# Gate product in plain float32 over four column groups, and a new table of stage offsets

## The chip, the cores and the metric

The kernel runs on one core of one Trainium2 chip. The core has a matrix engine (TensorE, PE in the profile, with its weight loads as PEld), a vector engine (VectorE, DVE), a scalar engine (ScalarE, ACT), GpSimd (POOL), and SyncE (SP), which here issues the loads and stores. The metric is device time in microseconds (us), lower is better. The kernel before took 2730.89 us, the median of three runs (2729.17 to 2732.62).

## The reference

One layer of a decoder over 2048 tokens of width 1024 in float32: a gated DeltaNet mixer with 8 heads of 128 and chunks, a memory cross-attention with 4 heads beside it, an output projection, a layer norm, an MLP with squared ReLU and 4096 hidden units, and a second layer norm. What matters here is the gate part: 16 of the columns of the input projection, 8 for `a` and 8 for `b`.

```python
def gdn_mixer(x, mem_k, mem_v, w_in, conv_w, a_log, dt_bias, gate_norm_w, w_out):
    proj = x @ w_in
    qkv = proj[..., :3 * GDN_WIDTH]
    z = proj[..., 3 * GDN_WIDTH:4 * GDN_WIDTH]
    a = proj[..., 4 * GDN_WIDTH:4 * GDN_WIDTH + GDN_HEADS]
    b = proj[..., 4 * GDN_WIDTH + GDN_HEADS:4 * GDN_WIDTH + 2 * GDN_HEADS]
    ...
    beta = jax.nn.sigmoid(b.astype(jnp.float32))
    g = -jnp.exp(a_log) * jax.nn.softplus(a.astype(jnp.float32) + dt_bias)
    o = chunk_gated_delta_rule(q, k, v, g, beta)
```

## The kernel before, in words

The tokens are worked through in four blocks of 512 (TB), two blocks to a pass s. For each pass the main loop (line 1809) runs `mixer` for both blocks, then `out_seven` (output projection and first norm), `ff1` and `ff2` (the MLP and second norm). Matrices of 1024 rows are handled in eight pieces k of 128 rows (KT = 8).

**Precision.** The large products run on float32r operands (a float32 type that the matmul reads at reduced precision). To keep float32 accuracy, `split` (line 555) writes each operand as a high part, by a copy on ScalarE, and a low part, by a subtraction on VectorE; `mm3` (line 573) then issues three matmuls: high·high, high·low, low·high. The split tokens of a block are the tiles T (line 649): 4 high and 4 low tiles of two k each, all eight buffers of the tag `tt`. The next block's T can be written only as the present block's last product with T has read them. Products of the recurrence (`pc`, `po` in `gdn_b`, line 1064) and transposes are plain float32.

**The order of the work.** Nothing is issued directly. Every call on an engine is recorded by `Recorder` (line 206) with a cost (line 272), the buffers that it needs and what it depends on. `issue` (line 313) then goes through all recorded operations on a modelled clock: at each engine the one that is ready and has the lowest priority number goes next; the number is the order of recording plus `shift` plus `base`. `spot` (line 529) sets `base` from the table `PLACE` (line 190), which holds an offset for some stages, named by block, step and letter (B and A are the two halves of the recurrence of a head, D its projections, Z its gate z, M memory attention, F a part of the MLP, X and W operands and weights of the output projection). A buffer of a tag is given out in the order of its users' first recorded use. The modelled clock decides the order alone; the times here are all from the chip.

**The gate product.** `gates(b, T)` (line 726) loads the 16 columns of weights (`abraw`), splits them into high and low halves side by side in `abw`, a stationary tile of 32 columns, and issues for each k two matmuls, against the high and the low part of T:

```python
            nc.tensor.matmul(a[:32], w[:, k], T_of(T, 0, k), start=k == 0, stop=False)
            nc.tensor.matmul(a[:32], w[:, k], T_of(T, 1, k), start=False, stop=k == KT - 1)
```

The result `aab` has 32 rows by 512 tokens: the products with the high weights and with the low weights. It is copied out by ScalarE (`ab`), transposed in four pieces to tokens by 32 (`pab`), and the two halves of 16 columns are added into `gab`. The rest of `gates` works out the decay and beta from it; that part is not changed.

**Where it stands.** For block 0 the tokens come in `first_tokens` (line 1587), piece by piece, each with its split, into two-piece tiles of the tag `tok`; `columns` loads the norm weights, and `gates` follows (line 1820). For the later blocks `next_block(b, step)` (line 1608) runs steps 0 to 4: steps 0 to 3 load two k of x each (`xj`, a buffer of the tag `wraw`, of which there are three) and split them into T; step 4 loads the first weights and calls `gates`. For odd blocks (1 and 3) these steps are recorded behind the mixer of the block before; for block 2 they are recorded in `ff2` of the first pass, during its last product (line 1561), whose own operands are in slots of the tags `d` (11 buffers) and `s0` (14 buffers).

Of the kernel before, what the change touches and what calls it, by code (L numbers as in the profile page):

```python
# [8 lines left out]
F32 = mybir.dt.float32  # L9
# [5 lines left out]
P = 128  # L15
# [4 lines left out]
H = 8  # L20
# [164 lines left out]
class Op:  # L185
# [2 lines left out]


PLACE = {  # L190
# [12 lines left out]
}  # L203


class Recorder:
# [65 lines left out]
    def cost(o, name, wr, rd, args, kw):  # L272
# [3 lines left out]
        if e == "PE":  # L276
            rhs = kw.get("rhs", args[2])
            mo, n = _prod(args[1].shape[1:]), _prod(rhs.shape[1:])
            f32 = name == "transpose" or isinstance(rhs, Ref) and rhs.buf.dtype == F32
            o.load, o.cols, o.lhs = 4 + 0.84 * mo, mo, args[1].buf if isinstance(args[1], Ref) else None  # L280
            o.last = 2.4 + 0.8334 * n if f32 else 13.4 + 0.4167 * n
            if name == "transpose":
                return o.last
            if f32:
                return o.last + max(o.last, o.load)
            return o.last
# [154 lines left out]
def hybrid_layer(  # L441
# [46 lines left out]
    def small(name, shape, bufs=3, dt=F32):  # L488
        return rec.buf(sm, shape, dt, name, bufs, name)
# [42 lines left out]
    state = [rec.buf(cst, (P, P), F32, "state%d" % h, 1, "state") for h in range(H)]  # L532
    for h in range(H):
        nc.gpsimd.memset(state[h], 0.0)
    lnc = rec.buf(cst, (P, 4 * KT), F32, "lnc", 1, "lnc")
    nea = rec.buf(cst, (P, H), F32, "nea", 1, "nea")
    halo = rec.buf(cst, (P, 24, 3), F32, "halo", 1, "halo")
# [185 lines left out]
                                  in_=st[i].bitcast(F32).rearrange("p (h e) -> p h e", h=MH))  # L723


    def gates(b, T):
        raw = small("abraw", [P, KT, 16], 1)
        nc.sync.dma_start(out=raw, in_=w_ab.rearrange("p (k f) -> p k f", k=KT))
        w = small("abw", [P, KT, 32], 1, F32R)
        split(raw, w[:, :, :16], w[:, :, 16:])  # L730
        a = bank("aab", "acc")
        for k in range(KT):
            nc.tensor.matmul(a[:32], w[:, k], T_of(T, 0, k), start=k == 0, stop=False)
            nc.tensor.matmul(a[:32], w[:, k], T_of(T, 1, k), start=False, stop=k == KT - 1)
        ab = slot("ab", "th")
        nc.scalar.copy(out=ab[:32], in_=a[:32])
        pab = bank("pab", "m")
        for c in range(NC):
            nc.tensor.transpose(pab[:, c * 32:(c + 1) * 32], ab[:32, c * P:(c + 1) * P], ident[:32, :32])
        pc = pab[:, :P].rearrange("p (c f) -> p f c", c=NC)  # L740
        pv = small("gab", [P, 16, NC], 1)
        nc.vector.tensor_copy(pv, pc[:, 16:])
        nc.vector.tensor_tensor(out=pv, in0=pc[:, :16], in1=pv, op=ALU.add)
        sh = [P, H, NC]
        if b == 0:
            alog = small("alog", [P, H], 1)
# [838 lines left out]
        nc.vector.tensor_copy(lnc, pt[:, :4 * KT])  # L1585

    def first_tokens():
        T = T_tiles()
        rt = rec.buf(wp, (P, KT, P), F32, "wraw", NR, "wraw")
        wt, hi, lo = pair()  # L1590
        hi, lo = hi.rearrange("p (k f) -> p k f", k=KT), lo.rearrange("p (k f) -> p k f", k=KT)
        for k in range(KT):
            if k % 2 == 0:
                xj = tok_tile("xj").rearrange("p (k f) -> p k f", k=2)
            if k in W0K:
                w = slice(k, W0K[k])
                kw = range(k, W0K[k])
                nc.sync.dma_start(out=rt[:, w].part(*kw), in_=w_in[0].rearrange("p (k f) -> p k f", k=KT)[:, w])
                split(rt[:, w].part(*kw), hi[:, w].part(*kw), lo[:, w].part(*(100 + i for i in kw)))
            xk = xj[:, k % 2].part(k % 2)  # L1600
            nc.sync.dma_start(out=xk, in_=xtd[:, k, 0:TB])
            split(xk, T_of(T, 0, k), T_of(T, 1, k))
        nc.sync.dma_start(out=wsc[0], in_=wt.bitcast(F32))
        return T, ([hi[:, k].part(k) for k in range(KT)], [lo[:, k].part(100 + k) for k in range(KT)])

# [2 lines left out]
    def next_block(b, step):  # L1608

        if b >= NB:  # L1610
            return
        if step < 4:
            if step == 0:
                ahead["T"] = T_tiles()
            k = 2 * step
            xj = rec.buf(wp, (P, 1024), F32, "wraw", NR, "xj").rearrange("p (k f) -> p k f", k=2)
            nc.sync.dma_start(out=xj, in_=xtd[:, k:k + 2, b * TB:(b + 1) * TB])
            split(xj, *(t[step] for t in ahead["T"]))
        else:
            ahead["w0"] = load_in(b, 0)  # L1620
            ahead["G"] = gates(b, ahead["T"])


    def mixer(b, T, w0, G):
# [184 lines left out]
    for s in range(NB // 2):  # L1809
        x1d = [rec.buf(dr, (P, D), F32, "x1d%d" % t, 1, "x1d") for t in range(2 * NC)]  # L1810
        T0d = rec.buf(dr, (P, KT, TB), F32, "T0d", 1, "T0d")
        for n in ("A11", "A12", "A22", "S1", "S2", "S3", "S4"):
            xo[n] = rec.buf(dr, (P, 6, TB), F32, "xo" + n, 1, "xo")
        inv = inverse_tiles()
        for i in range(2):
            b = 2 * s + i
            if b == 0:
                T, w0 = first_tokens()
                columns()
                G = gates(b, T)  # L1820
            else:
                T, w0, G = ahead["T"], ahead["w0"], ahead["G"]
            mixer(b, T, w0, G)
            if i == 0:
                for k in range(5):
                    next_block(b + 1, k)
        ys, T = out_seven(s, x1d, T0d)
        ff1(s, ys, T0d, first_half(T))
        ff2(s, x1d)
# [56 lines left out]
```

## Time and profile before

| | |
|---|---|
| median of three runs | 2730.89 us |
| the profiled execution's own time | 2731.02 us |
| its span, first to last instruction | 2729.3 us |
| TensorE busy, matmuls | 2707.3 us (99%), 13605 records |
| TensorE weight loads | 2265.5 us (83%) |
| VectorE busy | 2106.6 us (77%) |
| ScalarE busy | 1634.3 us (60%) |
| GpSimd busy | 414.5 us (15%) |
| mean granted TensorE clock | 0.999 |

The profile is one execution recorded by the hardware. Its page gives busy time for each engine and the chain of work that ended last; views of the trace give groups of instructions, what an engine waited for, the timeline of instructions, and busy time in chosen stretches. Rows of the timeline merge neighbours of one kind: start, length from the first start to the last end, engine, line, operation, output<-inputs, shape, count, and in brackets how long the engine sat idle before and what ended that. As all operations pass through the recorder, they all show its line 424, so they are told apart by the names of their tiles. Numbers of a group `x64: 387/396/479` are least, median and greatest duration in ns. float32r operands show as f32 on TensorE.

### The profile page before, as it was taken

The numbers are of one execution on the slowest core, as the hardware profiler recorded it, in microseconds if no ns is written. First come the engines' busy times: TensorE is split into PE (matmuls) and PEld (weight loads), VectorE is DVE, ScalarE is ACT, GpSimd is POOL, SyncE is SP. The second block draws the span as 40 slices with busy tenths as digits, with TensorE's granted clock in tenths as the row PEclk, the third lists the DMA queues.
The fourth block names the chain that finished last, engine by engine and source line by source line (L and its number), as shares of the span: only waits on it lengthen the run. The fifth ranks groups of instructions, "written<-read, shape, count | busy, mean of one in ns | idle before, by whom it ended". The sixth has DMA issues, their size and how long they took to land.

```text
span 2729.3 us, 42448 instructions
## 1 busy us (share of the span) xinstructions
PE 2707.3 (99%) x13605; PEld 2265.5 (83%) x13605; DVE 2106.6 (77%) x5644; ACT 1634.3 (60%) x4106; POOL 414.5 (15%) x1030
## 2 busy tenths in 40 slices
PE   9999999999999999999999999999999999999998
PEld 7888888888888888888888888888887888888887
DVE  7999889998877777655778887888878666567575
ACT  7778767776475555333446676777756655553341
POOL 3233223321000000000023221332201000000000
PEclk9999999999999999999999999999999999999999
DMA  8666548867787879765754445345678643476673
GB/s 321 232 222 229 206 177 293 309 244 267 264 307 282 296 271 311 261 219 194 263 212 147 140 163 185 140 147 173 217 264 287 228 165 137 162 277 224 212 237 114
DMA packets 208543, 613.99 MB, mean 225 GB/s; under 512 B 23072, under 2 KB 32192, under 8 KB 188352
## 3 DMA queue, kind: packets, MB, share of 16 engines
q1 hardware_dynamic: 207888, 611.23, 63.7%
q8 instruction: 107, 1.75, 0.3%
q14 instruction: 116, 0.95, 0.1%
q10 hardware_dynamic: 432, 0.05, 0.0%
HBM read 436.54 MB, written 174.65 MB: 224 GB/s over the span
## 4 chain that ended last, share of the span: by engine, by line
PE 92%; DVE 3%; ACT 3%; POOL 1%; issue 1%; DMA 1%; DVEq 0%; SPq 0%; POOLq 0%; ACTq 0%
PE f2A L424 13%; PE fA L424 13%; PE ao L424 8%; PE f2C L424 6%; PE fC L424 6%; PE av L424 6%; PE aq L424 6%; PE ak L424 6%; PE az L424 5%; PE f2B L424 3%; PE fB L424 3%; PE amq L424 3%; PE pc L424 3%; PE po L424 2%; PE pkq L424 2%; PE pq L424 1%
## 5 line engine op out<-in xcount | busy, mean ns | idle before, releaser
L424 DVE TENSOR_TENSOR whl<-wraw,whl 128x512 fp32r<-128x512 f32 (+2 forms) x294 | 257.0, 884 | 112.5 <-ACT whl L424 109.6
L424 ACT CAST whl<-wraw 128x512 fp32r<-128x512 f32 (+2 forms) x294 | 226.6, 780 | 158.6 <-PE fC L424 54.6
L424 PE MATMUL fA<-B,whl 128*128 128x512 f32 x1152 | 278.9, 389 | 0.0
L424 ACT CAST X<-X 128x1024 fp32r<-128x1024 f32 x118 | 123.9, 1052 | 231.2 <-DMA X<-xsc 203.2
L424 PE MATMUL f2A<-whl,X 128*128 128x512 f32 x1152 | 262.1, 389 | 0.0
L424 PEld LDWEIGHTS fA<-B,whl 128*128 128x128 f32 x1152 | 216.1, 188 | 45.3 <-DVE B L424 0.3
L424 PEld LDWEIGHTS f2A<-whl,X 128*128 128x128 f32 x1152 | 216.3, 188 | 44.8
L424 DVE TENSOR_TENSOR X<-X,X 128x1024 fp32r<-128x1024 f32 x118 | 144.0, 1221 | 128.8 <-ACT X L424 128.8
L424 PE MATMUL aq<-T,whl 128*128 128x512 f32 x768 | 216.5, 409 | 6.5 <-ACT T L424 5.5
L424 PE MATMUL av<-T,whl 128*128 128x512 f32 x768 | 221.9, 405 | 1.0 <-DVE Bc L424 1.0
L424 PE MATMUL az<-T,whl 128*128 128x512 f32 x768 | 222.8, 404 | 0.0
L424 PE MATMUL ak<-T,whl 128*128 128x512 f32 x768 | 210.8, 405 | 0.0
L424 PE MATMUL fC<-B,whl 128*128 128x512 f32 x768 | 186.8, 389 | 0.4 <-DVE B L424 0.4
L424 PE MATMUL f2C<-whl,X 128*128 128x512 f32 x768 | 174.7, 389 | 0.0
L424 PEld LDWEIGHTS fC<-B,whl 128*128 128x128 f32 x768 | 144.0, 188 | 31.0 <-DVE B L424 0.8
L424 PEld LDWEIGHTS f2C<-whl,X 128*128 128x128 f32 x768 | 144.2, 188 | 29.9
L424 PEld LDWEIGHTS aq<-T,whl 128*128 128x128 f32 x768 | 136.8, 191 | 28.7 <-ACT T L424 5.5
L424 PEld LDWEIGHTS av<-T,whl 128*128 128x128 f32 x768 | 137.8, 189 | 24.2 <-ACT mst L424 1.4
L424 PEld LDWEIGHTS ak<-T,whl 128*128 128x128 f32 x768 | 137.3, 189 | 23.5
L424 PEld LDWEIGHTS az<-T,whl 128*128 128x128 f32 x768 | 137.9, 189 | 22.3
L424 POOL TENSOR_SCALAR ve<-mv 128x1 f32<-128x1 f32 x34 | 16.8, 493 | 918.3 <-DVE mv L424 917.8
L424 PE MATMUL ao<-whl,X 128*128 128x512 f32 x528 | 139.9, 404 | 0.3 <-DVE whl L424 0.3
(294 smaller groups left out, 6294.3 us busy)
## 6 DMA issues: line engine op xcount, KB each, us to landing
whl<-wsc SPq DMA_DIRECT2D x108, 1024.0 KB, 4.9
wraw<-in_w_ff_dram SPq DMA_DIRECT2D x106, 512.0 KB, 4.4
X<-xsc SPq DMA_DIRECT2D x96, 512.0 KB, 3.9
wsc<-whl SPq DMA_DIRECT2D x36, 1024.0 KB, 6.5
whl<-tsc SPq DMA_DIRECT2D x64, 512.0 KB, 4.6
xsc<-hB SPq DMA_DIRECT2D x96, 256.0 KB, 3.8
xo<-cat SPq DMA_DIRECT2D x80, 256.0 KB, 4.3
wraw<-in_w_in_dram SPq DMA_DIRECT2D x35, 512.0 KB, 6.0
```

The lines of the kernel that those rows point to most:

```text
L424: o.fn(*[res(a) for a in o.args], **{k: res(v) for k, v in o.kw.items()})
```

## The change

The gate product takes x itself instead of its split. The weights `abw` are one constant tile, 8 pieces of 32 columns in plain float32, cleared once; the 16 columns are loaded once in `first_tokens`, and the other 16 of each piece stay zero. `gate_rows` issues one matmul for each k, and writes it to the output rows 32·(k mod 4) to 32·(k mod 4) + 31 of `aab`, which puts it on another group of 32 columns of the array for each of four neighbouring k; k and k + 4 accumulate in the same rows. `gates` then copies all 128 rows, transposes four full 128 by 128 pieces, and adds the four groups by a reduction for each piece.

For block 0 `first_tokens` records all eight matmuls behind the splits. In `next_block`, odd blocks load x as before and record the matmuls in two batches of four, at steps 1 and 3; block 2 loads each k by itself into a slot of the tag `s0` and records all eight in one batch at step 3. The bank of `aab` is asked for at step 0. The cost function gets a line for such matmuls, a quarter of the usual float32 cost. `PLACE` is replaced as a whole.

```diff
--- before.py
+++ after.py
@@ -188,18 +188,19 @@
 
 
 PLACE = {
-    ('w',): 445, (0, 0, 'F'): -65, (0, 1, 'Y'): 285, (0, 2, 'D'): -5, (0, 2, 'Y'): -225, (0, 2, 'n'): 600,
-    (0, 5, 'A'): 175, (0, 5, 'M'): -20, (0, 6, 'A'): -145, (0, 6, 'B'): -200, (0, 6, 'D'): 90, (0, 6, 'Z'): 325,
-    (0, 7, 'B'): -600, (0, 7, 'D'): -170, (0, 8, 'B'): -430, (1, 2, 'D'): 335, (1, 3, 'A'): 150, (1, 3, 'B'): 300,
-    (1, 3, 'D'): 245, (1, 3, 'K'): -185, (1, 4, 'A'): -160, (1, 5, 'A'): 160, (1, 5, 'Z'): 210, (1, 6, 'A'): 45,
-    (1, 6, 'B'): -550, (1, 6, 'D'): -165, (1, 6, 'F'): -45, (1, 7, 'Z'): -60, (2, 1, 'Z'): -60, (2, 3, 'A'): 340,
-    (2, 4, 'A'): 10, (2, 5, 'A'): -40, (2, 5, 'B'): 100, (2, 5, 'M'): -140, (2, 6, 'D'): -600, (2, 6, 'M'): 120,
-    (2, 7, 'A'): 10, (2, 7, 'D'): 295, (2, 8, 'A'): -10, (2, 8, 'B'): -225, (2, 8, 'M'): -100, (2, 8, 'Z'): -440,
-    (3, 2, 'A'): -195, (3, 2, 'B'): -530, (3, 2, 'D'): 360, (3, 3, 'B'): 235, (3, 3, 'D'): 140, (3, 3, 'Z'): -110,
-    (3, 4, 'A'): 25, (3, 4, 'B'): 250, (3, 5, 'A'): -460, (3, 5, 'D'): 20, (3, 5, 'Z'): -80, (3, 6, 'D'): 70,
-    (3, 6, 'Z'): 20, (3, 7, 'B'): -315, (3, 7, 'Z'): 315, (3, 8, 'Z'): 115, (0, 0, 2, 'X'): 150, (0, 1, 0, 'X'): 140,
-    (0, 5, 1, 'X'): 225, (0, 5, 2, 'X'): 155, (0, 6, 0, 'W'): -150, (1, 0, 0, 'W'): -355, (1, 1, 2, 'W'): -600,
-    (1, 5, 0, 'X'): 10, (1, 5, 2, 'W'): -375, (1, 6, 0, 'W'): 15, (1, 6, 2, 'X'): -25,
+    (0, 0, 'F'): -410, (0, 0, 'H'): -270, (0, 1, 'D'): -120, (0, 1, 'H'): -130, (0, 1, 'Y'): -75, (0, 1, 'Z'): -130,
+    (0, 12, 'F'): 160, (0, 13, 'F'): 50, (0, 2, 'A'): 340, (0, 2, 'D'): -235, (0, 2, 'n'): 215, (0, 3, 'A'): -285,
+    (0, 3, 'Z'): -165, (0, 4, 'Z'): 25, (0, 5, 'D'): 125, (0, 5, 'F'): 55, (0, 5, 'M'): -25, (0, 5, 'Z'): -400,
+    (0, 6, 'A'): 40, (0, 6, 'F'): 10, (0, 6, 'M'): -165, (0, 7, 'A'): 125, (0, 7, 'M'): 80, (0, 7, 'Z'): 105,
+    (0, 8, 'A'): 300, (0, 9, 'B'): 235, (0, 9, 'F'): -150, (1, 2, 'A'): -295, (1, 3, 'K'): 205, (1, 3, 'Z'): 320,
+    (1, 4, 'B'): -160, (1, 4, 'D'): 15, (1, 4, 'K'): -595, (1, 4, 'O'): 495, (1, 4, 'Z'): -35, (1, 5, 'B'): 215,
+    (1, 5, 'D'): 20, (1, 5, 'O'): 390, (1, 5, 'Z'): -40, (1, 6, 'M'): 345, (1, 6, 'O'): 245, (1, 6, 'Z'): -215,
+    (1, 7, 'D'): 20, (1, 7, 'M'): 50, (1, 7, 'Z'): -215, (1, 9, 'B'): -130, (2, 1, 'D'): -25, (2, 1, 'Z'): -60,
+    (2, 2, 'A'): 190, (2, 2, 'D'): 75, (2, 2, 'Z'): -355, (2, 3, 'A'): -110, (2, 3, 'B'): 20, (2, 5, 'A'): 245,
+    (2, 5, 'D'): 110, (2, 5, 'M'): 190, (2, 6, 'Z'): -220, (2, 7, 'A'): -180, (2, 7, 'M'): 325, (2, 8, 'B'): -360,
+    (2, 8, 'Z'): 445, (3, 1, 'A'): 90, (3, 1, 'D'): -175, (3, 2, 'B'): -400, (3, 5, 'M'): -10, (3, 6, 'B'): -220,
+    (3, 6, 'Z'): -105, (3, 7, 'A'): -60, (3, 7, 'B'): 40, (0, 4, 0, 'W'): -600, (1, 4, 2, 'X'): -300,
+    (1, 5, 1, 'W'): -160, (1, 6, 0, 'W'): 180, (1, 6, 1, 'W'): -375,
 }
 
 
@@ -281,6 +282,8 @@
             o.last = 2.4 + 0.8334 * n if f32 else 13.4 + 0.4167 * n
             if name == "transpose":
                 return o.last
+            if f32 and mo == 32 and n == 512:
+                return (o.last + max(o.last, o.load)) / 4
             if f32:
                 return o.last + max(o.last, o.load)
             return o.last
@@ -532,6 +535,8 @@
     state = [rec.buf(cst, (P, P), F32, "state%d" % h, 1, "state") for h in range(H)]
     for h in range(H):
         nc.gpsimd.memset(state[h], 0.0)
+    abw = rec.buf(cst, (P, KT, 32), F32, "abw", 1, "abw")
+    nc.gpsimd.memset(abw, 0.0)
     lnc = rec.buf(cst, (P, 4 * KT), F32, "lnc", 1, "lnc")
     nea = rec.buf(cst, (P, H), F32, "nea", 1, "nea")
     halo = rec.buf(cst, (P, 24, 3), F32, "halo", 1, "halo")
@@ -723,24 +728,21 @@
                                   in_=st[i].bitcast(F32).rearrange("p (h e) -> p h e", h=MH))
 
 
-    def gates(b, T):
-        raw = small("abraw", [P, KT, 16], 1)
-        nc.sync.dma_start(out=raw, in_=w_ab.rearrange("p (k f) -> p k f", k=KT))
-        w = small("abw", [P, KT, 32], 1, F32R)
-        split(raw, w[:, :, :16], w[:, :, 16:])
-        a = bank("aab", "acc")
-        for k in range(KT):
-            nc.tensor.matmul(a[:32], w[:, k], T_of(T, 0, k), start=k == 0, stop=False)
-            nc.tensor.matmul(a[:32], w[:, k], T_of(T, 1, k), start=False, stop=k == KT - 1)
+    def gate_rows(a, xs, ks):
+        for k, x in zip(ks, xs):
+            q = slice(32 * (k % 4), 32 * (k % 4) + 32)
+            nc.tensor.matmul(a[q], abw[:, k], x, start=k < 4, stop=k >= 4)
+
+    def gates(b, a):
         ab = slot("ab", "th")
-        nc.scalar.copy(out=ab[:32], in_=a[:32])
+        nc.scalar.copy(out=ab, in_=a)
         pab = bank("pab", "m")
         for c in range(NC):
-            nc.tensor.transpose(pab[:, c * 32:(c + 1) * 32], ab[:32, c * P:(c + 1) * P], ident[:32, :32])
-        pc = pab[:, :P].rearrange("p (c f) -> p f c", c=NC)
+            nc.tensor.transpose(pab[:, c * P:(c + 1) * P], ab[:, c * P:(c + 1) * P], ident)
         pv = small("gab", [P, 16, NC], 1)
-        nc.vector.tensor_copy(pv, pc[:, 16:])
-        nc.vector.tensor_tensor(out=pv, in0=pc[:, :16], in1=pv, op=ALU.add)
+        for c in range(NC):
+            nc.vector.tensor_reduce(out=pv[:, :, c], in_=pab[:, c * P:(c + 1) * P].rearrange("p (j f) -> p f j", j=4)[:, :16],
+                                    op=ALU.add, axis=AX.X)
         sh = [P, H, NC]
         if b == 0:
             alog = small("alog", [P, H], 1)
@@ -1585,7 +1587,7 @@
         nc.vector.tensor_copy(lnc, pt[:, :4 * KT])
 
     def first_tokens():
-        T = T_tiles()
+        T, xs = T_tiles(), []
         rt = rec.buf(wp, (P, KT, P), F32, "wraw", NR, "wraw")
         wt, hi, lo = pair()
         hi, lo = hi.rearrange("p (k f) -> p k f", k=KT), lo.rearrange("p (k f) -> p k f", k=KT)
@@ -1600,6 +1602,10 @@
             xk = xj[:, k % 2].part(k % 2)
             nc.sync.dma_start(out=xk, in_=xtd[:, k, 0:TB])
             split(xk, T_of(T, 0, k), T_of(T, 1, k))
+            xs.append(xk)
+        nc.sync.dma_start(out=abw[:, :, :16], in_=w_ab.rearrange("p (k f) -> p k f", k=KT))
+        ahead["ab"] = bank("aab", "acc")
+        gate_rows(ahead["ab"], xs, range(KT))
         nc.sync.dma_start(out=wsc[0], in_=wt.bitcast(F32))
         return T, ([hi[:, k].part(k) for k in range(KT)], [lo[:, k].part(100 + k) for k in range(KT)])
 
@@ -1611,14 +1617,28 @@
             return
         if step < 4:
             if step == 0:
-                ahead["T"] = T_tiles()
+                ahead["T"], ahead["x"], ahead["ab"] = T_tiles(), [], bank("aab", "acc")
             k = 2 * step
-            xj = rec.buf(wp, (P, 1024), F32, "wraw", NR, "xj").rearrange("p (k f) -> p k f", k=2)
-            nc.sync.dma_start(out=xj, in_=xtd[:, k:k + 2, b * TB:(b + 1) * TB])
-            split(xj, *(t[step] for t in ahead["T"]))
+            c = slice(b * TB, (b + 1) * TB)
+            if b % 2:
+                xj = rec.buf(wp, (P, 1024), F32, "wraw", NR, "xj").rearrange("p (k f) -> p k f", k=2)
+                nc.sync.dma_start(out=xj, in_=xtd[:, k:k + 2, c])
+                split(xj, *(t[step] for t in ahead["T"]))
+                ahead["x"] += [xj[:, j] for j in range(2)]
+                batch = 4
+            else:
+                for j in range(2):
+                    xj = slot("xj", "s0")
+                    nc.sync.dma_start(out=xj, in_=xtd[:, k + j, c])
+                    split(xj, *(T_of(ahead["T"], i, k + j).part(j) for i in range(2)))
+                    ahead["x"].append(xj)
+                batch = KT
+            n = len(ahead["x"])
+            if n % batch == 0:
+                gate_rows(ahead["ab"], ahead["x"][n - batch:], range(n - batch, n))
         else:
             ahead["w0"] = load_in(b, 0)
-            ahead["G"] = gates(b, ahead["T"])
+            ahead["G"] = gates(b, ahead["ab"])
 
 
     def mixer(b, T, w0, G):
@@ -1817,7 +1837,7 @@
             if b == 0:
                 T, w0 = first_tokens()
                 columns()
-                G = gates(b, T)
+                G = gates(b, ahead["ab"])
             else:
                 T, w0, G = ahead["T"], ahead["w0"], ahead["G"]
             mixer(b, T, w0, G)
```

## The prediction

> **What bounds the kernel now.** I read the page first, then stretches of the span, then the waits of TensorE.
>
> ```profile
> span 2729.3 us, 42448 instructions
> PE 2707.3 (99%) x13605; PEld 2265.5 (83%) x13605; DVE 2106.6 (77%) x5644; ACT 1634.3 (60%) x4106; POOL 414.5 (15%) x1030
> PE 92%; DVE 3%; ACT 3%; POOL 1%; issue 1%; DMA 1%; DVEq 0%; SPq 0%; POOLq 0%; ACTq 0%
> ```
>
> TensorE (PE) is busy for 99% of the span, and 92% of the chain that ended last is its own instructions. So a matmul that goes away is worth what it occupied, and one that comes costs the same, wherever it stands. Next, busy time by stretch; the columns are the length, then PE, PEld, DVE, ACT, POOL, the clock.
>
> ```profile
> 14.00:320.00 306.00, 302.01 (x1704) 255.97 (x1702) 273.09 (x966) 238.69 (x730) 97.91 (x233) 1.00 0.68 243
> 320.00:690.00 370.00, 369.13 (x2093) 312.98 (x2092) 330.43 (x1223) 258.48 (x853) 98.21 (x245) 1.00 0.73 257
> 690.00:1360.00 670.00, 669.30 (x2978) 551.80 (x2977) 481.83 (x686) 344.37 (x508) 17.48 (x34) 1.00 0.77 267
> 1360.00:1680.00 320.00, 320.00 (x1772) 271.75 (x1771) 254.49 (x948) 204.47 (x701) 91.05 (x237) 1.00 0.46 166
> 1680.00:2050.00 370.00, 369.68 (x2065) 314.95 (x2064) 314.05 (x1179) 248.66 (x815) 86.45 (x224) 1.00 0.54 190
> 2050.00:2718.00 668.00, 666.63 (x2968) 550.65 (x2968) 435.58 (x610) 331.50 (x488) 15.12 (x28) 1.00 0.59 205
> ```
>
> PE's idle time between 14 and 2718 us is 3.99 + 0.87 + 0.70 + 0 + 0.32 + 1.37 = 7.25 us. That is all an order of the work could still win by closing gaps, so it bounds from above what the new table of offsets gives. The rest of the 22 us of idle time lies in the first load and in the last tokens' normalization, which the change leaves alone. The clock column is 1.00 throughout.
>
> **What is removed.** The gate product, tile aab, is 64 matmuls on a stationary tile of 32 columns.
>
> ```profile
> L424 PEld LDWEIGHTS aab<-T,abw x64: 107/108/112, 13.4 to 1673.5; 128*32 128x32 f32 x64
> L424 PE MATMUL aab<-T,abw x64: 387/396/479, 13.6 to 1673.7; 128*32 128x512 f32 x64
> L424 ACT COPY ab<-aab x4: 575/576/577, 17.6 to 1674.1; 32x512 f32<-32x512 f32 x4
> ```
>
> A duration of 396 ns is not a cost: it includes the way through the array, which overlaps the next matmul. The cost is the distance between starts, and the timeline gives it where the 16 stand together, at the end of the MLP ahead of block 2:
>
> ```profile
> 1358.67 0.39 PE L424 MATMUL f2A<-whl,xl 128*128 128x512 f32 x1
> 1358.67 3.53 PEld L424 LDWEIGHTS aab<-T,abw 128*32 128x32 f32 x16
> 1358.90 3.82 PE L424 MATMUL aab<-T,abw 128*32 128x512 f32 x16
> 1362.55 0.61 PE L424 MATMUL f2A<-whl,xh 128*128 128x512 f32 x2
> ```
>
> From 1358.90 to 1362.55 is 3.65 us, 0.228 us each. In block 0 the same 16 stand from 13.64 to 17.38, which is 3.74 us:
>
> ```profile
> 13.64 3.90 PE L424 MATMUL aab<-T,abw 128*32 128x512 f32 x16
> 17.38 1.32 PE L424 MATMUL ak<-T,whl 128*128 128x512 f32 x5
> ```
>
> I take 3.7 us for each of four blocks: 14.8 us of PE go.
>
> **What is added.** Eight plain float32 matmuls for each block, 512 columns each. The trace has no such matmul, but it shows how a plain float32 one runs, and how long its pieces are:
>
> ```profile
> 1664.61 0.39 PE L424 MATMUL pc<-state,ck 128*128 128x128 f32 x2
> 1664.83 0.39 PE L424 MATMUL po<-state,qd 128*128 128x128 f32 x2
> 1669.74 0.60 PE L424 MATMUL ptq<-ident,cq 128*128 128x128 f32 x4
> L424 PE MATMUL pc<-state,ck x256: 270/273/377, 53.9 to 2021.2; 128*128 128x128 f32 x128
> ```
>
> Line 1072 issues the pc product 128 times (8 heads, 4 chunks, 4 blocks) and there are 256 records: each plain float32 matmul is two passes, one directly behind the other. From the pc pair to the po pair is 0.22 us, so 0.11 us for a pass of 128 columns; the transposes agree, (0.60 − 0.27)/3 = 0.11. A pass of 512 columns is not shown. From above it is 4 × 0.11 = 0.44 us; from below it is 0.227 us, the distance of the present matmuls over 512 columns. I take 0.44, since the rows it comes from have the same type.
>
> One block then has 16 passes, 7.04 us one after the other. The change puts product k on column group k mod 4, output partitions 32·(k mod 4) onward. Nothing in this trace shows two matmuls in different groups, so this is the unknown cost, with both ends: with no overlap 7.04 us, with all four groups at once 16 × 0.44/4 = 1.76 us. I take the latter, because the four products share neither array columns, stationary tile, streamed operand nor output partitions; it is an assumption, and two rivals rest on it. The start of each batch is staggered; the closest spacing of loads that I find is that of the pab transposes, about 0.06 us (0.32 us for four, of which the last takes 0.14):
>
> ```profile
> 1363.78 0.32 PEld L424 LDWEIGHTS pab<-ident,ab 32*128 32x128 f32 x4 [0.35 <-ACT abw L424]
> 1363.78 0.43 PE L424 MATMUL pab<-ident,ab 32*128 32x32 f32 x4
> 1364.14 0.50 PE L424 MATMUL f2A<-whl,xl 128*128 128x512 f32 x1
> 1364.48 0.62 PE L424 MATMUL f2A<-whl,xh 128*128 128x512 f32 x2
> ```
>
> Some 0.1 us a batch, and six batches (one each for blocks 0 and 2, two each for 1 and 3): 0.6 us. New cost 4 × 1.76 + 0.6 = 7.6 us. **PE: 14.8 − 7.6 = 7.2 us less.**
>
> The Trainium skill ("TensorEngine Tiling (Array Packing)", Key Properties) says that a change of tiling mode drains TensorE. The rows at 1358.67 show no drain: the first 32-column matmul starts 0.23 us behind a 128-column one. They may not be in a tiled mode, since they use one group. By that rule each batch would pay the overlapped part of a matmul, 0.39 − 0.227 = 0.16 us, twice: 12 × 0.16 = 1.9 us, an estimate, and the sum would be 5.3 us instead of 7.2.
>
> **The four transposes** of ab grow from 32 to 128 rows and columns. Now they and the matmul behind them take 1364.48 − 1363.78 = 0.70 us, of which that matmul is 0.23, so 0.47; four transposes of full size are 4 × 0.11 = 0.44. No change.
>
> **What lies beside PE.** The split of the gate weights goes (ACT 0.29 and DVE 0.28 us a block, and three of four loads of 64 KB); the copy and the addition of gab (0.22 us each) become four reductions of the same 64 elements, each bounded by that 0.22: DVE −0.28 − 0.44 + 0.88, so +0.2 us a block. For block 2 four loads of x of 512 KB become eight of 256 KB, four more SyncE issues of some 0.38 us, and the splits halve in width, which adds about 0.2 us of fixed time four times on ACT and on DVE. All this lies under PE: ACT is idle for 40% and DVE for 23%. Without that cover it would be some 3 us.
>
> **What is held longer.** A piece of x is now kept until its gate product has read it, not only until its split.
>
> ```profile
> 320.91 0.38 SPq L424 DMA_DIRECT2D xj<-in_xt_dram  x1
> 321.71 0.40 PE L424 MATMUL aab<-T,abw 128*32 128x512 f32 x1
> 322.73 1.87 PE L424 MATMUL aab<-T,abw 128*32 128x512 f32 x7
> 324.89 0.39 PE L424 MATMUL aq<-T,whl 128*128 128x512 f32 x1
> 327.39 1.32 PE L424 MATMUL aab<-T,abw 128*32 128x512 f32 x5
> ```
>
> For odd blocks x lies in three wraw buffers; the fourth piece is requested at 320.91, when a split has freed one. In the changed kernel the first four gate products must have run too, and these no longer wait for the split tiles T, so they can run earlier. Here the gate products also fill PE at the seam between blocks (7 and 5 in a row) while the last split is under way; with half their time gone, the query product aq of the new block moves up, whose first matmul already stands at 324.89. I price the seam at nothing, with that cover; without it, see the third rival. For block 2 x takes 8 of 14 s0 buffers beside the last product's operands; there PE is busy for 669.30 of 670 us, and I price it at nothing too.
>
> **The table** shifts priorities of whole stages. It removes no instruction. Its gain is at most the 7.25 us above, and a loss has no such bound; the largest single waits of PE between the ends give its grain:
>
> ```profile
> PE ao L424 <- ACT whl L424: 1.1, 1, 1.1
> PE aq L424 <- DVE whl L424: 1.0, 1, 1.0
> PE av L424 <- DVE Bc L424: 1.0, 1, 1.0
> ```
>
> A new order brings others of this size; I take nothing, plus or minus 4 us (four such waits).
>
> **Sum.** Against the profiled execution: 2731.0 us, its span of 2729.3 and 1.7 around it, less 7.2: 2723.8. The median of the runs, 2730.9, stands 0.1 lower: **2723.7 us**, 0.26% faster.
>
> **Rivals.**
>
> *The groups overlap by pairs only, or are broken up* (chance 0.22). The two passes of one product use the same group and are issued one behind the other, as the pc rows show. If the second pass holds up the queue until the first is through, only it and the next product's first pass run together: nine pass times for eight products, 9 × 0.44 = 3.96 us in one run, 2 × 5 × 0.44 = 4.4 in two batches; over the blocks 2 × 3.96 + 2 × 4.4 = 16.7 us against 14.8, so +1.9 us: 2732.8. Other instructions between the products of a batch would do the same; at 321.71 to 327.39 the gate product is broken up in this way. For: matmuls of this trace start in order. Against: nothing shows a pass waiting for its group alone. The Trainium skill ("TensorE: Matmul & The Clock Gate", Part 3, The mechanism) says that matmuls start and end strictly in program order and that tiles overlap; the first speaks for this rival, the second for the forecast, and no run here shows either.
>
> *No overlap* (0.13), the one on the other side: all 16 passes of a block in turn, 7.04 − 3.7 = 3.34 us more, four times, 13.4 us: 2744.3. It decides from the point where starts of aab passes stand more than 0.23 us apart on average (16 × 0.23 = 3.7). For: no two matmuls of this trace run at once. Against: none of them could have.
>
> *The seam stalls* (0.10). If the first batch is late in an odd block, the fourth piece of x comes late by a whole round: 4.6 us to land, 1.05 and 1.22 to split, 6.9 us, and PE runs out of other work. Twice 13.8, less 7.2: 2737.5.
>
> ```profile
> xj<-in_xt_dram SPq DMA_DIRECT2D x12, 512.0 KB, 4.6
> L424 ACT CAST T<-xj 128x1024 fp32r<-128x1024 f32 x12 | 12.6, 1057 | 3.8 <-DMA xj<-in_xt_dram 2.7 <-PE amq L424 1.0
> L424 DVE TENSOR_TENSOR T<-xj,T 128x1024 fp32r<-128x1024 f32 x12 | 14.6, 1221 | 2.0 <-ACT T L424 1.9
> ```
>
> Against: aq's matmuls on the first three pieces are ready then.
>
> **Chances and range.** The forecast has 0.55. Its own range is 2714 to 2731: low with 0.227 us a pass (4 × 0.91 + 0.6 = 4.2 us, so −10.6) and much of the idle time closed, high with the table's 4 us against it and the stagger larger than taken. The rivals at 2732.8 and 2737.5 lie above; of the one at 2744.3 I leave out about the half, so the range is 2714 to 2742. What a measurement of this kernel can tell from no change is 0.2%, 5.5 us, so the bounds are 2725.4 and 2736.4. Faster: 0.45 of the forecast's 0.55, 0.05 of the first rival, 0.01 of the third, 0.51. Slower: 0.01, 0.06, 0.12 and 0.06, 0.25. Within: 0.24.
>
> **What would show it.** In the changed profile: aab as 64 plain float32 records whose starts stand 0.11 us apart on average in a batch (forecast), 0.22 to 0.27 (pairs), 0.44 (none); PE's busy time down by about 7 us; no wait of aq on T of over 1 us near 325 and 1675 us; the idle time between 14 and 2718 us within 4 us of 7.25. The prediction is wrong if the groups do not overlap, or if PE's idle time in the mixers grows by more than the product saves.

## The result, and the profile after

The changed kernel takes 2725.47 us (median of 13 runs, 2724.22 to 2726.90); the kernel before took 2731.59 in the same sessions. The ratio is 0.9977, with a 95% interval of 0.9970 to 0.9984: 6.1 us less, a little under the 7.2 forecast. Its profiled execution has a span of 2722.9 us against 2729.3, so 6.4 less. The page, then busy time by stretch (length, then PE, PEld, DVE, ACT, POOL, the clock, DMA):

```profile
span 2722.9 us, 42463 instructions
PE 2703.4 (99%) x13605; PEld 2262.8 (83%) x13605; DVE 2106.7 (77%) x5652; ACT 1629.7 (60%) x4106; POOL 405.7 (15%) x1031
PE 94%; ACT 2%; DVE 2%; DMA 1%; issue 0%; POOL 0%; ACTq 0%; SPq 0%; DVEq 0%; POOLq 0%
```

```profile
14.00:320.00 306.00, 302.84 (x1701) 256.58 (x1697) 271.23 (x956) 240.63 (x727) 92.47 (x225) 1.00 0.68 242
320.00:690.00 370.00, 369.53 (x2097) 313.02 (x2097) 330.34 (x1237) 258.48 (x858) 102.08 (x255) 1.00 0.73 257
690.00:1360.00 670.00, 669.47 (x2990) 551.69 (x2989) 480.89 (x687) 339.37 (x506) 15.52 (x32) 1.00 0.77 267
1360.00:1680.00 320.00, 319.60 (x1774) 270.51 (x1773) 265.01 (x1026) 205.12 (x706) 88.48 (x245) 1.00 0.45 161
1680.00:2050.00 370.00, 369.96 (x2066) 316.83 (x2065) 310.02 (x1111) 249.75 (x814) 83.71 (x216) 1.00 0.57 200
2050.00:2713.70 663.70, 663.63 (x2957) 548.87 (x2955) 433.80 (x609) 328.42 (x486) 15.86 (x30) 1.00 0.60 204
```

PE's busy time fell by 3.9 us, not by the 7.2 that its instructions were to save. And the idle time between 14 us and the end of the matmuls fell from 7.25 to 4.67 (3.16 + 0.47 + 0.53 + 0.40 + 0.04 + 0.07), which the forecast had at no change. So the sum nearly came out, but not from the terms that it was made of. The gate product, first in block 2, where nothing comes between its matmuls:

```profile
1356.37 0.39 PE L427 MATMUL f2A<-whl,xl 128*128 128x512 f32 x1
1356.69 1.92 PE L427 MATMUL aab<-xj,abw 128*32 128x512 f32 x16
1358.54 0.74 PE L427 MATMUL f2A<-whl,xh 128*128 128x512 f32 x2
```

The 16 passes run from 1356.69 to 1358.54. Of this, 4 x 0.43 us are passes. The matmul before them has streamed after 0.227, at 1356.60, so 0.09 us goes by ahead of them; 0.09 more behind the last passes (it is within the 1.85); and the first matmul that follows holds the engine for 0.34 us (0.74 − 0.40) in place of 0.227, another 0.11. In all 2.06 us, against 3.65 before, and the 1.86 that the forecast took. Now block 1:

```profile
318.96 1.04 PE L427 MATMUL aab<-xj,abw 128*32 128x512 f32 x2
319.94 0.66 PE L427 MATMUL pq<-YP,inv 128*128 128x64 f32 x4
320.53 1.05 PE L427 MATMUL aab<-xj,abw 128*32 128x512 f32 x4
321.51 1.20 PE L427 MATMUL pmo<-pm,mkv 128*128 128x512 f32 x4
...
323.55 1.06 PE L427 MATMUL aab<-xj,abw 128*32 128x512 f32 x6
324.54 0.50 PE L427 MATMUL aq<-T,whl 128*128 128x512 f32 x1
...
328.89 1.05 PE L427 MATMUL aab<-xj,abw 128*32 128x512 f32 x4
329.88 0.63 PE L427 MATMUL sps<-mkv,mq 128*128 128x256 f32 x3
```

Here the eight products stand in parts of 1, 2, 3 and 2, two records each. Every part takes 0.98 us from its start to the next instruction, whether it holds one, two or three products, and 0.2 around it: 4.8 us for the block, where the kernel before paid 3.7. In block 3 the parts are 5, 1 and 2 products, and cost 4.4. The four transposes of a block stand like this in block 2:

```profile
1359.36 0.63 PE L427 MATMUL f2A<-whl,xh 128*128 128x512 f32 x2
1359.82 0.60 PE L427 MATMUL pab<-ident,ab 128*128 128x128 f32 x4
1360.17 0.47 PE L427 MATMUL f2A<-whl,xl 128*128 128x512 f32 x1
1360.49 0.63 PE L427 MATMUL f2A<-whl,xh 128*128 128x512 f32 x2
```

They and the matmul behind them take 1360.49 − 1359.82 = 0.67 us, of which that matmul is 0.227, so 0.45. Before, it was 0.47, and 0.1 us that passed ahead of them: 0.57. So TensorE pays 13.3 us for the gate product in place of 14.9, and 1.8 for the transposes in place of 2.3: **2.0 us of the 6.1 (6.4 in the span) are the product's own**. Some 2.6 are waits that are gone, and 1.9 of busy time lie in matmuls elsewhere that start closer together; they are taken up again below.

### The profile page after: what moved, and what is told of

Same layout as the page of the kernel before. It is cut to its first block, busy times and chain, and to the rows that moved or that the text cites. A ratio compares the mean times of both kernels' runs of the same rounds, so it can differ in the third digit from the quotient of the medians.

```text
span 2722.9 us, 42463 instructions
## 1 busy us (share of the span) xinstructions
PE 2703.4 (99%) x13605; PEld 2262.8 (83%) x13605; DVE 2106.7 (77%) x5652; ACT 1629.7 (60%) x4106; POOL 405.7 (15%) x1031
## 4 chain that ended last, share of the span: by engine, by line
PE 94%; ACT 2%; DVE 2%; DMA 1%; issue 0%; POOL 0%; ACTq 0%; SPq 0%; DVEq 0%; POOLq 0%
PE f2A L427 13%; PE fA L427 13%; PE ao L427 8%; PE fC L427 6%; PE f2C L427 6%; PE az L427 6%; PE av L427 6%; PE aq L427 6%; PE ak L427 5%; PE fB L427 3%; PE f2B L427 3%; PE amq L427 3%; PE pc L427 3%; PE po L427 2%; PE pkq L427 2%; PE pq L427 1%
## 5 line engine op out<-in xcount | busy, mean ns | idle before, releaser
L427 PE MATMUL av<-T,whl 128*128 128x512 f32 x768 | 214.9, 406 | 0.3 <-DVE whl L427 0.3
```

Of the source, the lines that this page charges most:

```text
L427: o.fn(*[res(a) for a in o.args], **{k: res(v) for k, v in o.kw.items()})
```

## The experiments

"Cost" of the gate product is read below as above, from the distances of starts, with what lies around each part. Every kernel was timed against the kernel before on its chip, whose median moved between 2730.7 and 2732.5.

### Each half of the change by itself

`table_only` is the kernel before with the new PLACE; `product_only` is the changed kernel with the old one (the same edit, the other way round).

```diff
-    ('w',): 445, (0, 0, 'F'): -65, (0, 1, 'Y'): 285, (0, 2, 'D'): -5, (0, 2, 'Y'): -225, (0, 2, 'n'): 600,
...
+    (0, 0, 'F'): -410, (0, 0, 'H'): -270, (0, 1, 'D'): -120, (0, 1, 'H'): -130, (0, 1, 'Y'): -75, (0, 1, 'Z'): -130,
...
```

> The kernel before with the new table of offsets alone; the gate product stays as before. Theory A (the product itself won only about 2 of the 6.1 us: 14.9 us of TensorE became 13.3, and the transposes 2.3 became 1.8; the rest came from the order): the time falls by about 4 us, to 2727.6, and TensorE's idle time between its first and last matmul falls from 7.25 us to about 5. Theory B (all of it is the product's doing, the table only keeps step): 2731.6, plus or minus 2. The gate product costs 14.9 us under both.

> The changed kernel with the old table of offsets. Theory A: 2731.6 less 2, so 2729.6, with idle time of TensorE near 7 us and the gate product at about 13 us. Theory B: 2725.5, as the changed kernel. An order for which neither table was drawn may add a few waits of about 1 us each.

Measured: 2750.55 us (ratio 1.0069, 1.0057 to 1.0082) and 2747.81 us (1.0061, 1.0048 to 1.0073). Both theories fall: either half alone is 15 to 18 us slower than the kernel before beside it (2732.47), and 22 to 25 slower than the changed kernel. The stretch from 14 to 2710 us as one row, of the changed kernel, of table_only and of product_only (PE busy is the third number):

```profile
14.00:2710.00 2696.00, 2691.33 (x13560) 2254.74 (x13557) 2088.04 (x5616) 1621.78 (x4092) 397.14 (x1000) 1.00 0.65 226
```

```profile
14.00:2710.00 2696.00, 2678.08 (x13446) 2240.28 (x13444) 2079.35 (x5589) 1623.47 (x4088) 403.22 (x996) 1.00 0.64 226
```

```profile
14.00:2710.00 2696.00, 2679.47 (x13459) 2235.83 (x13452) 2076.03 (x5599) 1624.91 (x4089) 401.22 (x996) 1.00 0.64 226
```

PE is idle for 4.7 us with the pair, 17.9 and 16.5 with either half, and the gate product costs 16.0 us in table_only (split into 19 parts, one of them with 0.6 us of idle time in it) and 13.6 in product_only. The clock adds to this: PE is busy for 14.4 us at half the granted clock in table_only (three stretches, from 447, 635 and 2048 us) and for 12.4 in product_only (two, from 83 and 643 us). Half of that, 7 and 6 us, is an estimate of what it costs beside the idle time. The product alone does not explain the slowdown. A table belongs to the set of operations that it was drawn for: it only shifts priorities, and when the operations are others, the same offsets give another order. The gain can't be shared out between product and table by leaving one out.

### A batch as one piece of work

`whole` records the four or eight matmuls of a batch as one operation of the planner, with the cost 0.3 us plus two passes for each four, so that nothing is put between them.

```diff
-        for k, x in zip(ks, xs):
-            q = slice(32 * (k % 4), 32 * (k % 4) + 32)
-            nc.tensor.matmul(a[q], abw[:, k], x, start=k < 4, stop=k >= 4)
+        ks, mm = list(ks), nc.tensor._real.matmul
+        def rows(o, *v):
+            for i, k in enumerate(ks):
+                mm(o[32 * (k % 4):32 * (k % 4) + 32], v[2 * i], v[2 * i + 1], start=k < 4, stop=k >= 4)
+        nc.add("PE", rows, "rows", (a, *(r for k, x in zip(ks, xs) for r in (abw[:, k], x))), {})
```

> The changed kernel, with each batch of four or eight gate products recorded as one piece of work, so that nothing comes between its matmuls; first all of its pieces of x must be there. Theory A (a batch that is broken up pays 0.86 us of passes and 0.3 us around them for each part): aab in the odd blocks falls from 4.8 and 4.4 us to 2.4 each, in all from 13.3 to 8.9 us, and the time by 4.4 us to 2721, give or take 2 for a new order. Rival (the parts stand where TensorE would wait anyway): the time stays at 2725.5 and idle time takes the place of the parts.

Measured: 2732.70 us (1.0000, 0.9991 to 1.0009), 7 us slower than the changed kernel. The product did what was expected: a batch of four takes 1.0 us and 0.2 around it, in block 1

```profile
320.30 1.07 PE L738 MATMUL aab<-xj,abw 128*32 128x512 f32 x8
321.30 0.66 PE L429 MATMUL ptv<-ident,cv 128*128 128x128 f32 x4
...
327.31 1.31 PE L738 MATMUL aab<-xj,abw 128*32 128x512 f32 x8
```

and 9.4 us in all against 13.3 (8.9 expected; the second batch of block 1 takes 0.5 more, with waits in and behind it). But PE's idle time from 14 to 2710 us rose from 4.7 to 12.3 us, most of it in waits of other products:

```profile
PE ao L429 <- DVE whl L429: 2.1, 4, 0.6
PE ao L429 <- ACT X L429: 1.9, 2, 1.2
PE aq L429 <- DVE whl L429: 1.4, 1, 1.4
PE pto L429 <- ACT on L429: 1.3, 1, 1.3
```

So the rival, that idle time would take the place of the parts, gave the nearer time; but the waits stand in the output projection (ao) and elsewhere, not where the parts were. The table was the changed kernel's, for another set of operations.

### One column group

`one_group` puts all products on the first 32 columns (with copy, transposes and cost to match).

```diff
-            q = slice(32 * (k % 4), 32 * (k % 4) + 32)
-            nc.tensor.matmul(a[q], abw[:, k], x, start=k < 4, stop=k >= 4)
+            q = slice(0, 32)
+            nc.tensor.matmul(a[q], abw[:, k], x, start=k == 0, stop=k == KT - 1)
```

> The changed kernel with all eight gate products of a block on one column group, accumulated in 32 rows; copy and transposes of 32 rows as in the kernel before. Theory (the overlap of four groups is what makes plain float32 cheap): starts 0.43 us apart, 16 passes of a block in 6.9 us, 27.6 us in all against 13.3: 2725.5 plus 14 is 2740. Rival (plain float32 passes of one group overlap each other, or fill time in which TensorE would wait): under 2732.

Measured: 2760.31 us (1.0104, 1.0090 to 1.0117), 20 more than expected. The product costs 33.0 us, so 20 of the 35 us over the changed kernel; the rest goes with a new order: PE idle 16.1 us from 14 to 2710, and 9.2 us of busy time at half the granted clock. To separate the two, `one_group_same_order` keeps the planner's costs of product, transposes and reduction as they are in the changed kernel, so that every engine gets its work in the very same order, and `two_groups_same_order` does this with k mod 2. The traces bear this out: all 13605 matmul records come in the changed kernel's order of tiles, and so do the instructions of ACT, POOL and, but for the sums of gab, DVE.

```diff
             mo, n = _prod(args[1].shape[1:]), _prod(rhs.shape[1:])
+            if wr[0].buf.name == "pab":
+                n = P
...
         if e == "DVE":
+            if wr[0].buf.name == "gab":
+                n = 64
```

> All eight gate products of a block on one column group, as in one_group, but with the planner's costs held at those of the changed kernel, so that every engine gets its work in the changed kernel's order; only the overlap goes. Theory (four groups at once is what the product wins): blocks 0 and 2 pay 16 passes of 0.43 us and 0.3 around them, 7.2 us each; the odd blocks 6.9 us of passes and 0.3 for each of 4 and 3 parts, 8.1 and 7.8; in all 30.3 us against 13.3, so 2725.5 + 17 = 2742.5. Rival (the 35 us that one_group was slower by came from the product, not from its order): about 2760.

> The same with two column groups, k mod 2. Theory (a group runs its passes in turn, and groups run beside each other): blocks 0 and 2 take 8 x 0.43 + 0.3 = 3.7 us each; in the odd blocks parts of 1, 2, 3 and 2 products, and of 5, 1 and 2, take 5.5 and 5.2; in all 18.1 us against 13.3: 2730.3. Rival (the two passes of a product hold up the queue, so that a second group hides only one pass): the passes pair off as they do with four groups under that rival, and two groups cost what four do, 2725.5.

Measured: 2742.06 us (1.0036, 1.0024 to 1.0048) and 2729.74 us (0.9993, 0.9984 to 1.0002), each within 0.6 us of what was expected. In block 2, one group and then two:

```profile
1363.30 7.05 PE L431 MATMUL aab<-xj,abw 128*32 128x512 f32 x16
1370.29 0.73 PE L431 MATMUL f2A<-whl,xh 128*128 128x512 f32 x2
```

```profile
1358.74 3.63 PE L431 MATMUL aab<-xj,abw 128*32 128x512 f32 x16
1362.30 0.73 PE L431 MATMUL f2A<-whl,xh 128*128 128x512 f32 x2
```

From start to the next matmul: 6.99, 3.56, and 1.85 us with four groups. A group runs its passes in turn, 0.43 us each, and groups run fully beside each other. In all the product costs 30.4 and 18.4 us (30.3 and 18.1 expected) against 13.3, and the time follows: with the order held, 17.1 and 5.1 us more of gate product are 16.6 and 4.3 us more of kernel. The rivals, that the two passes of a product hold up the queue or that one group is cheap, are ruled out.

### Tables drawn for their own operations

A random search over the offsets, scored by the kernel's planning clock alone, drew a table for the kernel before (`before_drawn`) and two for `whole` (`whole_drawn`, `whole_drawn_2`). For the latter, `next_block` also got offsets for its steps.

```diff
+        spot(b, step, "N")
         if step < 4:
...
             if n % batch == 0:
+                spot(b, step, "g")
                 gate_rows(ahead["ab"], ahead["x"][n - batch:], range(n - batch, n))
         else:
             ahead["w0"] = load_in(b, 0)
+            spot(b, step, "g")
             ahead["G"] = gates(b, ahead["ab"])
+        spot(None)
```

> The kernel before, gate product and all, with a table of offsets drawn anew for its own set of operations (a random search on the kernel's planning clock, no chip). Theory C (a table belongs to the operations it was drawn for; a good part of the changed kernel's gain is that its table was drawn further, and the gate product as such gives some 2 us): 2728, plus or minus 2, with TensorE's idle time between its first and last matmul under 7 us. Rival (the old table was as good as a table gets; the gain needs the product): 2732 or more.

> The kernel whole with a table drawn for its operations by the same search. Theory C: its 7 us over the changed kernel came from a table that was drawn for another set; with one of its own the 4 us that whole batches save on TensorE show: aab 9.4 us in all, idle time about 5 us, 2722, plus or minus 2. Rival (whole batches need their pieces of x at once and stall the seams, whatever the order): 2728 or more, with waits near the seams at 320, 1360 and 1665 us.

> The same with a second table from another start of the search, equally good on the planning clock. It shows how far two tables of one worth there differ on the chip: under 2 us if the planning clock is a good guide, 5 or more if a table has to be tried on the chip. Otherwise as whole_drawn: 2722 or 2728.

Measured: 2732.00 us (1.0002, 0.9993 to 1.0011), 2728.61 us (0.9989, 0.9980 to 0.9998) and 2726.74 us (0.9983, 0.9974 to 0.9992). The kernel before gained nothing from a new table (PE idle 8.1 us from 14 to 2710, where under 7 was expected): for it the rival was right, at least as far as this search reaches. With tables of its own `whole` came down by 4 and 6 us (3 and 5 if each is set against the kernel before beside it), and the product stayed at 9.0 and 8.9 us; but it was not below the changed kernel. For whole_drawn the rival gave the nearer time, but not for its reason, a stall of the seams: behind the start, no wait of PE is longer than 0.8 us. The trace shows where 3 us of it went. The first matmuls of whole_drawn_2:

```profile
8.64 0.80 PE L600 MATMUL aq<-T,whl 128*128 128x512 f32 x1 [8.64 <-ACT T L600]
9.23 0.63 PE L600 MATMUL ak<-T,whl 128*128 128x512 f32 x1
```

PE starts at 8.64 us; in the changed kernel it starts at 5.46. SyncE requested weights of the next products ahead of the first x:

```profile
0.79 1.34 SPq L600 DMA_DIRECT2D wraw<-in_w_in_dram  x3
2.17 1.21 SPq L600 DMA_DIRECT2D xj<-in_xt_dram  x2
```

The changed kernel requests its first weights at 0.79 and x at 1.24:

```profile
0.79 0.39 SPq L427 DMA_DIRECT2D wraw<-in_w_in_dram  x1
1.24 0.89 SPq L427 DMA_DIRECT2D xj<-in_xt_dram  x2
```

So a third table was drawn with these first requests held in place (`whole_drawn_3`), and run beside the changed kernel:

> Whole batches with a third table, drawn under the condition that the first block's first weights and x are requested before anything else (with the tables of whole_drawn and whole_drawn_2 the first matmul started at 8.7 us, with the changed kernel's at 5.5). Theory C: aab stays at 9 us, the first matmul starts at 5.5 us, so whole_drawn_2 less 3.2: 2723.5, plus or minus 2, which is 2 below the changed kernel. Rival (a table that mends the start gives the 3 us back as waits in the mixers): 2725.5 or more, no gain over the changed kernel.

> The changed kernel itself, on the chip of whole_drawn_3, so that the two can be set side by side: 2725.5, plus or minus 1.

Measured: 2722.35 us (0.9971, 0.9959 to 0.9982; 2721.61 to 2724.02 in six runs), and for the changed kernel 2725.23 us (0.9982, 0.9973 to 0.9991; 2724.01 to 2728.52 in eleven). On this chip the two ranges only touch (2724.02 against 2724.01); the intervals of the ratios overlap, so that it is the faster of the two by 2.9 us is likely rather than certain. It is faster than the kernel before by 8.4. Its page, and its gate product in block 2:

```profile
span 2720.5 us, 42453 instructions
PE 2699.6 (99%) x13605; PEld 2261.8 (83%) x13605; DVE 2101.7 (77%) x5652; ACT 1628.1 (60%) x4106; POOL 409.1 (15%) x1031
```

```profile
1355.47 1.93 PE L905 MATMUL aab<-xj,abw 128*32 128x512 f32 x16
1357.32 0.74 PE L596 MATMUL f2A<-whl,xh 128*128 128x512 f32 x2
```

PE is busy for 4.1 us less than in the run of the changed kernel beside it (2703.7). The product costs 9.6 against 13.3 us there, 3.7 less, and the first matmul starts at 5.60 us. It is the best of three tables, and its search had offsets that the changed kernel's table lacks; the changed kernel was not given such a search, so what the whole batches win by themselves is not shown by the time alone.

## Why the prediction came out, point by point

**The bound.** Right: PE stays at 99%, and with the order held the time follows the product's cost nearly one for one (one_group_same_order: 17.1 us more product, 16.6 us more time).

**What was removed, and the price of a pass.** Right: 14.9 us went (14.8 predicted), and a pass of 512 columns costs 0.43 us (0.44).

**The overlap.** The assumption on which the forecast stood is shown: four groups run at once. The rival in which the two passes of a product hold up the queue, and the one without overlap, are ruled out by the pair with the same order.

**"Six batches", and "I price the seam at nothing".** This is the step that failed. The added cost was 13.3 us, not 7.6, so the term of 7.2 us was 1.5, and 2.0 with the transposes. The sum took two whole batches in an odd block; the planner, which charges a product a quarter of its passes wherever it stands, put other matmuls between them, four and three parts in place of two. A part of one product costs what one of four does. Of the 5.7 us by which the sum was short, 3.3 are passes: the parts of an odd block take eight rounds of 0.43 us where two whole batches take four. The other 2.4 are entries and exits, nine in place of six, and 0.3 us each in place of 0.1. Against the kernel before, the odd blocks lost 1.1 and 0.7 us, and blocks 0 and 2 won 1.6 each. The prediction named the break-up as the second half of its first rival ("or are broken up"), but priced it by the first half, passes in pairs: 4.4 us for an odd block, which is near the 4.8 and 4.4 measured, and 3.96 for blocks 0 and 2, which took 2.06. So that price fits the odd blocks by luck; passes do not pair off. The Trainium skill's page "TensorEngine Tiling (Array Packing)", Key Properties, has a drain at each change of tiling mode; the estimate made from it, 0.16 us twice, is close to what the trace now shows (0.09 ahead, 0.09 behind and 0.11 in the next matmul). It should have stood in the sum. It was left out because a lone group showed no drain; one_group_same_order, with plain float32 in a lone group, has the same 0.09 us ahead:

```profile
1362.99 0.39 PE L431 MATMUL f2A<-whl,xl 128*128 128x512 f32 x1
```

That matmul has streamed after 0.227, at 1363.21, and the gate product starts at 1363.30. So it is not the number of groups that decides.

**The transposes.** No change predicted, 0.5 us less in all: the small ones too have 0.1 us around them on each side. The working took the one behind, 0.34 − 0.227 in the next matmul, and missed the one ahead: the matmul before them starts at 1363.46, has streamed at 1363.68, and they start at 1363.78. That this is a change of mode as well is likely, but no run tests it.

**What lies beside PE, and what is held longer.** Nothing came of it: PE waits for the tiles T in the changed kernel only for its first matmul (5.5 us) and once more for 0.2 us, at 6.45 us, both in block 0's first load:

```profile
PE aq L427 <- ACT T L427: 5.5, 1, 5.5
PE ptv L427 <- ACT Y L427: 1.0, 4, 0.4
...
PE aq L427 <- DVE T L427: 0.2, 1, 0.2
```

So the rival of the stalled seam didn't come about.

**The table.** Predicted at nothing plus or minus 4 us, measured at a gain of about 4 (4.1 by the medians; in the span 2.6 of idle time and 1.9 of matmuls that stand closer, rounded). That is at the edge of what was allowed, and it made up for the product's shortfall: that the total came within 1.8 us of the forecast is luck. Of the signs that the prediction gave, the starts (0.12 us apart in block 2) and the idle time held, and PE's busy time, "down by about 7 us", did not.

The 1.9 us are for the most part waits too. A matmul of 512 columns is recorded for 0.39 us but streams in 0.227, so the last one ahead of a wait counts 0.16 us of it as busy. From 14 us on PE has 22 waits in the kernel before and 16 in the changed one: six times 0.16 is 1.0 us, an estimate. A wait shorter than 0.16 us hides altogether: between float32r matmuls of 512 columns with no recorded wait, distances of 0.25 to 0.39 us in place of 0.227 occur 17 times before and 4 times after, which is another 1.3 us. Together this is a little more than the 1.9. By this estimate, what the new order brought is fewer waits.

But "the table" is not a separate term, as table_only and product_only show: a change of the operations with the old table costs 15 us against the kernel before, and the new one is worth having only with them. Why these waits are fewer under this table was not traced to single offsets, and stays open.

## What to carry to other kernels

When a planner fills TensorE from a priority list, tell it that products on neighbouring column groups belong together: as one piece of work four cost one part, about 1.0 us here, and one by itself costs the same. Hold the order of issue fixed (by keeping the planner's costs) before you price an edit in a list-scheduled kernel; here another table alone, with the operations as they were, cost 18 us (table_only) and 22 us (product_only), more than the edit was worth. And what a search on a planning clock finds must be checked against the trace, here at the first loads.

## What the runs showed of the hardware

**Four column groups run at the same time, each with its own passes in turn.** In the changed kernel the 16 records of one batch start in four rounds, some 0.43 us apart (the row of 1356.69: 1.92 us for 16 records of 0.59, so (1.92 − 0.59)/0.43 = 3 steps). The first passes of four products start together, and then the second ones: a group with a pass under way does not hold up its neighbours. If the two passes of a product are issued one behind the other, as the prediction took it, they do not start in that order; the order of issue itself is not in the trace. The Trainium skill ("TensorE: Matmul & The Clock Gate", Part 3, Measured speedup vs the span model) adds some 4 ns for each further tile that runs beside the first; here the four starts of a round spread over 0.02 us, some 7 ns from one to the next, which is of that order.

**Plain float32 products on 32 columns have a gap of 0.09 us ahead of them; plain float32 alone, or 32 columns alone, has none.** The 0.09 us pass with four groups (1356.69) as with one (1363.30). Ahead of float32r products on 32 columns, at 1358.67 in the kernel before, nothing passes (0.23 us from start to start), and nothing ahead of plain float32 transposes on 128 columns either (the row of 1359.82: the second matmul of the row before it starts at 1359.59, 0.23 us earlier).

**Behind waits the granted clock can halve for some us.** In table_only, PE waits for 3.58 us from 445, and its clock is halved from 447.1 to 453.9; in the row of 447 to 454 the granted clock is the 0.51 behind the busy times:

```profile
448.68 0.47 PE L425 MATMUL pto<-ident,on 128*128 128x128 f32 x1 [3.58 <-ACT on L425]
```

```profile
440.00:447.00 7.00, 5.10 (x27) 3.90 (x25) 6.62 (x19) 3.75 (x14) 5.62 (x4) 1.00 1.00 327
447.00:454.00 7.00, 5.32 (x16) 4.28 (x17) 3.31 (x11) 4.15 (x13) 3.08 (x5) 0.51 0.27 97
454.00:461.00 7.00, 7.00 (x44) 6.12 (x43) 5.18 (x19) 4.55 (x18) 0.83 (x2) 1.00 0.83 293
```

PE is busy for 5.3 us of the halved stretch, so some 2.6 us, an estimate, are lost besides the 3.6 of the wait. A wait this long is not needed: in product_only the longest one behind the start is 2.34 us, up to 83.07, and behind it the clock is halved for 10.2 us:

```profile
83.00:94.00 11.00, 9.63 (x24) 6.79 (x25) 11.00 (x56) 3.29 (x5) 1.35 (x1) 0.53 0.51 170
```

In `whole` it is halved from 629.4 to 632.8 with no wait of over 1.5 us behind the start, so these runs give no threshold. The kernel before and the changed one stay at 1.00 from 11 us to the end of their matmuls; this is one reason why an order with more waits costs more than their sum.
